# Hi/lo splits of streamed weights: all on the Vector engine, none on GpSimd

## The chip, the core and the metric

One core of a Trainium2 chip runs the whole program. The metric is device time in microseconds (us) for one execution; the profiled execution is taken by the hardware profiler. Engines are named as in the profile: PE is TensorE's matmuls, DVE is VectorE, ACT is ScalarE, POOL is GpSimd, SP issues the loads.

## What is computed

A trunk of four post-norm layers over 512 tokens of width 1024, in float32. Layer 0 mixes tokens with latent attention (MLA), layer 1 with retention, layer 2 with gated linear attention (GLA), layer 3 with MLA again. A SwiGLU feed-forward network (FFN, hidden width 2816) follows each mixer. Cut to what matters:

```python
for i in range(4):
    y = (mla, retention, gla)[i % 3](x)
    x = layer_norm(ALPHA * x + y)
    x = layer_norm(ALPHA * x + (silu(x @ Wg) * (x @ Wu)) @ Wo)
```

So there are eight sub-layers, and seven places where one sub-layer's LayerNorm is followed by the next sub-layer's first products.

## The kernel before

Every float32 product is made of three fast products. An operand x is split into hi (a rounded copy) and lo = x - hi, and `mm3` (L127) issues hi·hi, lo·hi and hi·lo into one PSUM sum (L128, L129, L130). Activations are split once, when they are made: x is kept transposed as `xh` and `xl`. Weights stream from memory and are split as they come. `wload` (L106) takes one of three raw buffers (`wraw`, `nraw=3`), has SP load 512 KB into it, and calls `wsplit` (L116): ACT copies to `whi` (L102), then a subtraction writes `wlo` (L103). There are six pairs of `whi` and `wlo` (`nhl=6`). A raw buffer is free for the next load when its subtraction is done, and a pair is free when the last matmul on it is done.

The subtraction runs on DVE, except for some weights that `wsplit` gives to POOL, by a counter:

```python
self.split(hi, lo, raw, self.nc.gpsimd if self.relieve > 0 else None)
self.relieve -= 1
```

The counter `relieve` is set to 6 at the end of a sub-layer (L228 in `out_proj`, the short output projection of retention, GLA and FFN; L260 in `out_tail`, that of MLA) and to 2 in three turns of GLA's loop over heads (L1060). The next so many weights go to POOL: six behind each of seven sub-layers (behind the eighth there are no weights left) and two in each of three turns of GLA, 48 in all. POOL's other work (four additions per pair of FFN columns, L329 to L332; part of retention's output, L899 and L900; the root of MLA's normalisation; set-up of GLA, L950 to L960 and L1077) does not depend on the counter.

LayerNorm works on four tiles of 128 tokens. When the last output sum of a tile is ready in PSUM, DVE adds it into `xt` (`acc`, L182 or L184) and takes statistics (L186). `ln_finish` then runs on DVE: mean and variance (L191), a reciprocal root as a chain of one-column steps (L141 to L149, tiles `lnx`, `lny`, `lnu`), two steps (x - mean)·g (L205, 512 columns each) and two steps ·r + b (L206). Then PE transposes the tile (L158), ACT copies it to `xh`, and DVE subtracts to get `xl` (L103). The next sub-layer's first products on that tile need `xh`, `xl` and the split weights. The work is staggered: while tile 2 or 3 is normalised, PE ends the old sub-layer or works on the tiles that are done.

The order of each engine's queue is fixed when the program is built: a scheduler goes through the program with its own estimate of durations and puts the next ready instruction into its engine's queue. On the chip every engine works its queue in that order and waits for what an instruction needs.

Of the kernel before, what the change touches and what calls it, by code (L numbers as in the profile page):

```python
# [9 lines left out]
F32 = mybir.dt.float32  # L10
# [3 lines left out]
ALU = mybir.AluOpType  # L14
# [36 lines left out]
class Trunk:  # L51
    def __init__(self, tc, ctx, ins, nb=47, nraw=3, nhl=6):
        self.tc, self.nc, self.ins = tc, tc.nc, ins
        nc = tc.nc
        ctx.enter_context(nc.allow_non_contiguous_dma(reason="rows of weights and broadcasts"))
        pool = lambda name, bufs, **k: ctx.enter_context(tc.tile_pool(name=name, bufs=bufs, **k))
        self.cp = pool("cp", 1)
        self.wp = pool("wp", 1)
        self.nb = nb
        self.sp = pool("sp", 8)  # L60
        self.lnp = pool("lnp", 2)

        xp = pool("xp", 1)
        self.xh = xp.tile([P, KT, S], F32R, name="xh")
        self.xl = xp.tile([P, KT, S], F32R, name="xl")
        self.ps_pool = pool("psum", 6, space=bass.MemoryType.PSUM)
        self.nraw, self.nhl = nraw, nhl
        self.relieve = 0
        self.pending = []
        self.waiting = []  # L70

        self.ident = self.cp.tile([P, P], F32, name="ident")
        make_identity(nc, self.ident)
        self.xt = [self.cp.tile([P, D], F32, name=f"xt{t}") for t in range(NT)]
# [23 lines left out]
        return self.b(shape, F32R, "bh", tag), self.b(shape, F32R, "bl", tag)  # L98


    def split(self, hi, lo, src, eng=None):
        a = self.nc.scalar.copy(hi, src)  # L102
        b = (eng or self.nc.vector).tensor_tensor(lo, src, hi.bitcast(F32), op=ALU.subtract)  # L103
        return a.ins, b.ins

    def wload(self, srcs, a, n):  # L106
# [9 lines left out]
    def wsplit(self, raw, a, n):  # L116
        hi = self.wp.tile([P, a, n], F32R, tag="whi", name="whi", bufs=self.nhl)
        lo = self.wp.tile([P, a, n], F32R, tag="wlo", name="wlo", bufs=self.nhl)
        self.split(hi, lo, raw, self.nc.gpsimd if self.relieve > 0 else None)
        self.relieve -= 1  # L120
        return hi, lo

    def wcols(self, w, r0, kt, c0, n):
# [89 lines left out]
    def out_proj(self, st, w, nf, coef, last, out=None, halves=(0, 1)):  # L213
        wf = lambda f0, half: self.wcols(w, f0 * P, 2, half * 512, 512)
        if nf <= 6:
            ch = {(c, hf): wf(2 * c, hf) for hf in halves for c in range(nf // 2)}
            for t in range(NT):
                for hf in halves:
                    ps = self.ps()
                    for f in range(nf):  # L220
                        if last and hf == 0 and f == 3:
                            self.flush(t - 2)
                        w2 = ch[f // 2, hf]
                        self.mm3(ps, st(f, t), (w2[0][:, f % 2, :], w2[1][:, f % 2, :]), f == 0, f == nf - 1)
                    self.acc(t, hf, ps, coef, last)
                if last:
                    self.ln_finish(t, out)
            self.relieve = 6 if last else 0  # L228
            return
        pss = [self.ps() for _ in range(NT)]  # L230
        for f in range(nf):
            if f % 2 == 0:
                w2 = wf(f, 0)
            for t in range(NT):
                self.mm3(pss[t], st(f, t), (w2[0][:, f % 2, :], w2[1][:, f % 2, :]), f == 0, f == nf - 1)
        for t in range(NT):
            self.acc(t, 0, pss[t], coef, last)
        self.out_tail(st, lambda f0: wf(f0, 1), nf, coef, last, out)

    def out_tail(self, st, wf, nf, coef, last, out=None):  # L240

        pss = [self.ps() for _ in range(NT)]
        nl = 8
        for f in range(nf - nl):
            if f % 2 == 0:
                w2 = wf(f)
            for t in range(NT):
                self.mm3(pss[t], st(f, t), (w2[0][:, f % 2, :], w2[1][:, f % 2, :]), f == 0, False)
        ch = [wf(nf - nl + 2 * c) for c in range(nl // 2)]
        for t in range(NT):  # L250
            for c in range(nl):
                if last and c == 3:
                    self.flush(t - 2)
                f = nf - nl + c
                w2 = ch[c // 2]
                self.mm3(pss[t], st(f, t), (w2[0][:, c % 2, :], w2[1][:, c % 2, :]), f == 0, f == nf - 1)
            self.acc(t, 1, pss[t], coef, last)
            if last:
                self.ln_finish(t, out)
        self.relieve = 6  # L260


    def proj_f(self, w2, ps, kt, m, c=slice(None), mid=None):
# [680 lines left out]
    def gla(self, l, j):  # L944
# [22 lines left out]
        def values(h):  # L967

            v = self.bpair((P, 2, 256), "v"), self.bpair((P, 2, 256), "v")
            put = lambda t, ps: self.split(v[t // 2][0][:, t % 2], v[t // 2][1][:, t % 2], ps[:, :256])  # L970
            return [(v[t // 2][0][:, t % 2], v[t // 2][1][:, t % 2]) for t in range(NT)], 1024 + h * 256, put

        def gate(h):
            r = self.b((P, 2, 256), tag="r"), self.b((P, 2, 256), tag="r")
            return r, 2048 + h * 256, lambda t, ps: nc.scalar.copy(r[t // 2][:, t % 2], ps[:, :256])

        def project(*parts):
            ws = [self.proj_w(w, c0, 256, 4) for _, c0, _ in parts]
            for t in range(NT):
                for wk, (_, _, put) in zip(ws, parts):  # L980
                    self.proj_tile(t, wk, 256, put)
            return [p[0] for p in parts]
# [33 lines left out]
        def out(pr, yT, last, halves=(0, 1)):  # L1016
            if last:
                self.ln_begin(l, 0)
            st = lambda f, t: (yT[f][0][:, t * P : (t + 1) * P], yT[f][1][:, t * P : (t + 1) * P])
            coef = ALPHA if pr == 0 else None  # L1020
            self.out_proj(st, wo[pr * 512 : (pr + 1) * 512], 4, coef, last, halves=halves)

        def silu(r):
            for x in r:
                self.silu = self.tc.keep_in_program_order(nc.scalar.activation(x, x, AF.Silu))
# [17 lines left out]
        for h in range(GLA_H):  # L1043
            at, states = self._gla_scores(c, keys, v, fwd, crs)
            if h < 2:
                if h:
                    qk["q", h + 2] = q(h + 2)
                qk["k", h + 2] = k(h + 2)
            else:
                out(0, yT[:4], False, (h - 2,))  # L1050
            self._gla_mix(at, states, c[2:], v, r, ng)
            r0 = r
            if h + 1 < GLA_H:
                cs = gates(h + 1)
                c = self._gla_chain(cs, qk["q", h + 1], qk["k", h + 1])
                (v,) = project(values(h + 1))
            yT += self._gla_turn(r0)
            if h + 1 < GLA_H:
                (r,) = project(gate(h + 1))
                self.relieve = 2  # L1060
                keys = self._gla_keys(c)
                silu(r)
        out(1, yT[4:], True)
# [238 lines left out]
```

## Time and profile before

| | us |
|---|---|
| median of 3 runs (2597.5 to 2599.05) | 2598.49 |
| the profiled execution's own time | 2597.42 |
| its span, first to last instruction | 2595.6 |
| PE busy | 2539.5 |
| DVE busy | 1798.4 |
| ACT busy | 975.8 |
| POOL busy | 328.3 |

A row of the timeline gives start, duration, engine, line, operation, the tiles written and read, and in brackets how long the engine sat idle before it and what it waited for. "x2" means that two like instructions are merged, and the duration is that of both. A row of the windows gives for a stretch (from:to) its length, then each engine's busy time with its count of instructions, the granted clock of PE as a share of the full one (PEclk), the share of the DMA engines and GB/s.

### The profile page before, as it was taken

How to read it: one execution, taken by the hardware profiler on the slowest of the kernel's cores; microseconds unless marked ns; L12 is line 12 of the kernel's file. 1: busy time of each engine (PE TensorE's matmuls, PEld its weight loads, DVE VectorE, ACT ScalarE, POOL GpSimd, SP SyncE). 2: the span in 40 equal slices, each digit the busy share in tenths (PEclk: the TensorE clock that was granted, in tenths of full speed). 3: DMA queues.
4: the chain of work that ended last, by engine and by line, in shares of the span. 5: the costliest groups of instructions: out<-in, count | busy, mean ns of one | idle time of the engine just before them, and what ended most of it. 6: DMA issues, size and time to landing. Idle time of an engine off the chain costs nothing.

```text
span 2595.6 us, 32600 instructions
## 1 busy us (share of the span) xinstructions
PE 2539.5 (98%) x12804; PEld 2159.8 (83%) x12804; DVE 1798.4 (69%) x2932; ACT 975.8 (38%) x1405; POOL 328.3 (13%) x327
## 2 busy tenths in 40 slices
PE   8999999999999999999999999999999999999998
PEld 7788888887888887988888998888888788888886
DVE  6877766668655648666657888876657686676656
ACT  4652333323333332333323665233332564233331
POOL 3002111002100103111102001211101200211101
PEclk9999999999999999999999999999999999999999
DMA  4213333323222323323322222333332221333331
GB/s 146 74 42 94 106 98 97 102 77 98 81 82 77 102 75 89 114 91 107 111 94 83 82 66 74 110 98 98 97 90 79 78 68 47 117 97 98 98 90 57
DMA packets 294714, 232.36 MB, mean 90 GB/s; under 512 B 21120, under 2 KB 244480, under 8 KB 294560
## 3 DMA queue, kind: packets, MB, share of 16 engines
q1 hardware_dynamic: 294560, 230.28, 29.3%
q8 instruction: 100, 1.64, 0.3%
q14 instruction: 54, 0.44, 0.1%
HBM read 228.15 MB, written 2.10 MB: 89 GB/s over the span
## 4 chain that ended last, share of the span: by engine, by line
PE 88%; DVE 9%; ACT 2%; DMA 1%; POOL 1%; issue 1%; DVEq 0%; SPq 0%; ACTq 0%; POOLq 0%
PE ps L128 28%; PE ps L130 28%; PE ps L129 28%; DVE xt L205 2%; DVE xt L206 1%; PE tp L663 1%; DVE lnst L186 1%; PE tp L158 1%; DVE lnu L145 1%; PE ps L644 1%; DVE xt L182 1%; DVE xl L103 1%; PE ps L643 0%; DVE wlo L103 0%; ACT whi L102 0%
## 5 line engine op out<-in xcount | busy, mean ns | idle before, releaser
L102 ACT CAST whi<-wraw 128x1024 fp32r<-128x1024 f32 (+3 forms) x398 | 412.1, 1040 | 700.4 <-issue 251.6
L129 PE MATMUL ps<-xl,whi 128*128 128x512 f32 (+1 forms) x1792 | 659.1, 368 | 8.6 <-DVE xl L103 8.6
L128 PE MATMUL ps<-xh,whi 128*128 128x512 f32 (+1 forms) x1792 | 659.3, 368 | 0.0
L130 PE MATMUL ps<-xh,wlo 128*128 128x512 f32 (+1 forms) x1792 | 658.4, 367 | 0.0
L103 DVE TENSOR_TENSOR wlo<-wraw,whi 128x1024 fp32r<-128x1024 f32 (+2 forms) x350 | 431.1, 1242 | 204.8 <-ACT whi L102 197.2
L129 PEld LDWEIGHTS ps<-xl,whi 128*128 128x128 f32 x1792 | 340.1, 190 | 64.6 <-DVE xl L103 9.6
L128 PEld LDWEIGHTS ps<-xh,whi 128*128 128x128 f32 x1792 | 340.2, 190 | 55.0 <-issue 0.4
L130 PEld LDWEIGHTS ps<-xh,wlo 128*128 128x128 f32 x1792 | 340.1, 190 | 54.5
L130 PE MATMUL ps<-whi,xl 128*128 128x512 f32 (+3 forms) x752 | 265.2, 353 | 5.5 <-DVE xl L103 5.5
L128 PE MATMUL ps<-whi,xh 128*128 128x512 f32 (+3 forms) x752 | 267.0, 355 | 0.7 <-ACT xh L102 0.7
L129 PE MATMUL ps<-wlo,xh 128*128 128x512 f32 (+3 forms) x752 | 264.9, 352 | 2.0 <-POOL wlo L103 2.0
L103 POOL TENSOR_TENSOR wlo<-wraw,whi 128x1024 fp32r<-128x1024 f32 (+4 forms) x48 | 118.2, 2478 | 927.1 <-ACT whi L102 916.0
L182 DVE TENSOR_TENSOR xt<-ps,xt 128x512 f32<-128x512 f32 x288 | 187.3, 683 | 35.5 <-PE ps L130 35.5
L128 PE MATMUL ps<-whi,fh 128*128 128x512 f32 x448 | 174.3, 389 | 0.0
L129 PE MATMUL ps<-wlo,fh 128*128 128x512 f32 x448 | 174.3, 389 | 0.0
L130 PE MATMUL ps<-whi,fl 128*128 128x512 f32 x448 | 174.3, 389 | 0.0
L130 PEld LDWEIGHTS ps<-whi,xl 128*128 128x128 f32 x752 | 144.8, 193 | 23.7 <-DVE xl L103 6.5
L129 PEld LDWEIGHTS ps<-wlo,xh 128*128 128x128 f32 x752 | 144.8, 193 | 19.2 <-POOL wlo L103 2.2
L128 PEld LDWEIGHTS ps<-whi,xh 128*128 128x128 f32 x752 | 144.8, 193 | 18.5 <-ACT xh L102 1.1
L326 DVE TENSOR_TENSOR ft<-ps,b 128x512 f32<-128x512 f32 x64 | 44.2, 691 | 142.0 <-PE ps L130 77.8
L102 ACT CAST whi<-wt 128x1024 fp32r<-128x1024 f32 x64 | 67.5, 1054 | 190.9 <-PE ps L129 128.3
L128 PE MATMUL ps<-bh 128*128 128x256 f32 (+1 forms) x376 | 124.1, 335 | 6.0 <-ACT bh L102 5.5
(259 smaller groups left out, 4041.7 us busy)
## 6 DMA issues: line engine op xcount, KB each, us to landing
wraw<-in_ffn_w_in SPq DMA_DIRECT2D x176, 512.0 KB, 3.9
wt<-in_ffn_w_out SPq DMA_DIRECT2D x48, 512.0 KB, 4.7
wraw<-in_ret_w_in SPq DMA_DIRECT2D x48, 512.0 KB, 3.9
wraw<-in_ffn_w_out SPq DMA_DIRECT2D x40, 512.0 KB, 3.3
wraw<-in_gla_w_in SPq DMA_DIRECT2D x22, 512.0 KB, 3.6
wraw<-in_mla_w_o SPq DMA_DIRECT2D x16, 512.0 KB, 3.8
wraw<-in_ret_w_o SPq DMA_DIRECT2D x16, 512.0 KB, 4.7
wraw<-in_mla_w_down SPq DMA_DIRECT2D x8, 512.0 KB, 4.5
```

The costliest lines, as they stand in the source:

```text
L102: a = self.nc.scalar.copy(hi, src)
L103: b = (eng or self.nc.vector).tensor_tensor(lo, src, hi.bitcast(F32), op=ALU.subtract)
L128: mm(out, s[0], m[0], start=start, stop=False)
L129: mm(out, s[0], m[1], start=False, stop=False)
L130: mm(out, s[1], m[0], start=False, stop=stop)
L145: stt(u, y, y, x, op0=ALU.mult, op1=ALU.mult)
L158: nc.tensor.transpose(ps[:, j, :], self.xt[t][:, (4 * g + j) * P : (4 * g + j + 1) * P], self.ident)
L182: nc.vector.tensor_tensor(x, ps, x, op=ALU.add)
L186: nc.vector.bn_stats(self.stats[t][:, half * 6 : half * 6 + 6], x)
L205: nc.vector.scalar_tensor_tensor(x[:, sl], x[:, sl], mv[:, 0:1], self.g[:, sl], op0=ALU.subtract, op1=ALU.mult)
L206: nc.vector.scalar_tensor_tensor(x[:, sl], x[:, sl], r, self.bb[:, sl], op0=ALU.mult, op1=ALU.add)
L326: nc.vector.tensor_tensor(ft[:, 2:4, :] if f % 2 else ft[:, 1::-1, :], half(pu), half(s), op=ALU.mult)
```

## The change

The counter goes, and with it the choice of engine in `split`: all weights' subtractions are issued to DVE. LayerNorm and everything else stay as they are.

```diff
-        self.relieve = 0
...
-    def split(self, hi, lo, src, eng=None):
+    def split(self, hi, lo, src):
         a = self.nc.scalar.copy(hi, src)
-        b = (eng or self.nc.vector).tensor_tensor(lo, src, hi.bitcast(F32), op=ALU.subtract)
+        b = self.nc.vector.tensor_tensor(lo, src, hi.bitcast(F32), op=ALU.subtract)
         return a.ins, b.ins
...
     def wsplit(self, raw, a, n):
...
-        self.split(hi, lo, raw, self.nc.gpsimd if self.relieve > 0 else None)
-        self.relieve -= 1
+        self.split(hi, lo, raw)
...
-            self.relieve = 6 if last else 0
...
-        self.relieve = 6
...
-                self.relieve = 2
```

## Rows read from the trace of the kernel before

**Rows 1.** Windows: the end of the first MLA, and the FFN behind it.
```profile
205.00:262.00 57.00, 54.09 (x326) 47.70 (x325) 46.93 (x90) 14.49 (x19) 15.02 (x6) 1.00 0.35 107
262.00:585.00 323.00, 323.00 (x1503) 270.64 (x1502) 215.40 (x261) 106.81 (x115) 29.06 (x32) 1.00 0.32 97
```

**Rows 2.** Timeline of PE, the instructions behind its ten longest waits at these places.
```profile
242.90 0.39 PE L129 MATMUL ps<-xl,whi 128*128 128x256 f32 x1 [2.26 <-DVE xl L103]
...
615.78 0.80 PE L130 MATMUL ps<-whi,xl 128*128 128x512 f32 x1 [4.91 <-DVE xl L103]
...
1037.43 0.46 PE L129 MATMUL ps<-xl,whi 128*128 128x256 f32 x1 [3.42 <-DVE xl L103]
...
1398.71 0.40 PE L129 MATMUL ps<-wlo,xh 128*128 128x288 f32 x1 [1.96 <-POOL wlo L103]
...
1590.39 1.85 PE L1159 MATMUL tp<-ident,b 128*128 128x128 f32 x8 [1.81 <-DVE bl L103]
...
1616.84 0.44 PE L1240 MATMUL tp<-ident,b 128*128 128x128 f32 x2 [2.31 <-DVE b L1233]
...
1642.55 0.63 PE L158 MATMUL tp<-ident,xt 128*128 128x128 f32 x4 [1.77 <-DVE xt L206]
...
1654.39 1.43 PE L158 MATMUL tp<-ident,xt 128*128 128x128 f32 x8 [3.62 <-DVE xt L206]
...
2013.31 0.63 PE L158 MATMUL tp<-ident,xt 128*128 128x128 f32 x4 [2.13 <-DVE xt L206]
...
2232.44 0.58 PE L129 MATMUL ps<-xl,whi 128*128 128x256 f32 x1 [2.26 <-DVE xl L103]
```

**Rows 3.** Costliest groups of the page: the weights' subtraction on DVE and on POOL.
```profile
L103 DVE TENSOR_TENSOR wlo<-wraw,whi 128x1024 fp32r<-128x1024 f32 (+2 forms) x350 | 431.1, 1242 | 204.8 <-ACT whi L102 197.2
...
L103 POOL TENSOR_TENSOR wlo<-wraw,whi 128x1024 fp32r<-128x1024 f32 (+4 forms) x48 | 118.2, 2478 | 927.1 <-ACT whi L102 916.0
```

**Rows 4.** Two LayerNorm lines over the whole run: count, ns least/median/most.
```profile
L205 DVE SCALAR_TENSOR_TENSOR xt<-xt,lnmv,ln_g x61: 737/743/2939, 224.3 to 2588.4; 128x512 f32<-128x512 f32 x61
...
L145 DVE SCALAR_TENSOR_TENSOR lnu<-lny,lnx x32: 206/215/2356, 225.6 to 2589.1; 128x1 f32<-128x1 f32 x32
```

**Rows 5.** Timeline of DVE and POOL, from the first FFN to retention.
```profile
591.55 2.94 DVE L205 SCALAR_TENSOR_TENSOR xt<-xt,lnmv,ln_g 128x512 f32<-128x512 f32 x1
594.41 2.36 DVE L145 SCALAR_TENSOR_TENSOR lnu<-lny,lnx 128x1 f32<-128x1 f32 x1
...
602.46 5.12 DVE L206 SCALAR_TENSOR_TENSOR xt<-xt,lny,ln_b 128x512 f32<-128x512 f32 x2
...
591.53 9.94 POOL L103 TENSOR_TENSOR wlo<-wraw,whi 128x1024 fp32r<-128x1024 f32 x4 [110.28 <-ACT whi L102]
```

**Rows 6.** Timeline of DVE and POOL, from the first MLA to its FFN.
```profile
237.18 2.84 DVE L205 SCALAR_TENSOR_TENSOR xt<-xt,lnmv,ln_g 128x512 f32<-128x512 f32 x1
...
245.11 1.81 DVE L147 SCALAR_TENSOR_TENSOR lny<-lnu,lny 128x1 f32<-128x1 f32 x1
...
236.70 10.21 POOL L103 TENSOR_TENSOR wlo<-wraw,whi 128x1024 fp32r<-128x1024 f32 x4 [16.16 <-ACT whi L102]
```

**Rows 7.** Timeline of DVE, from GLA to its FFN.
```profile
1638.88 3.52 DVE L206 SCALAR_TENSOR_TENSOR xt<-xt,lny,ln_b 128x512 f32<-128x512 f32 x2
...
1644.90 2.88 DVE L205 SCALAR_TENSOR_TENSOR xt<-xt,lnmv,ln_g 128x512 f32<-128x512 f32 x1
```

**Rows 8.** Windows behind three of the waits, for the granted clock.
```profile
614.00:622.00 8.00, 6.22 (x19) 4.98 (x20) 2.92 (x5) 0.01 (x1) 0.00 (x0) 0.57 0.01 2
1037.00:1042.00 5.00, 4.57 (x25) 4.57 (x26) 5.00 (x11) 0.00 (x0) 2.08 (x1) 0.66 0.84 251
...
2232.00:2237.00 5.00, 4.56 (x26) 4.56 (x27) 4.89 (x7) 1.05 (x1) 4.44 (x2) 0.66 0.71 200
```

**Rows 9.** Waits of ACT for loads: 585 to 640 us, and whole run (total, times, longest).
```profile
ACT whi L102 <- DMA wraw<-in_ret_w_in: 7.4, 4, 2.7
...
ACT whi L102 <- DMA wraw<-in_ffn_w_in: 14.2, 6, 3.9
```

## The prediction

> **What bounds the kernel now.** I read the windows by stage first. Between the ends of sub-layers PE never rests: 323.00 of 323.00 us in the first FFN, at a full clock [rows 1]. There no other engine can add or save time, unless it becomes so late that PE waits. What is to be had lies at the ends and inside GLA, so I went through PE's timeline there and took the ten long waits [rows 2]. The reader is to see who is waited for: nine times DVE (the subtraction `xl`, the LayerNorm step L206 ahead of a transpose, two chains of GLA), once POOL's own subtraction `wlo`. They sum to 26.5 us: 2.26 + 4.91 + 3.42 + 1.96 + 1.81 + 2.31 + 1.77 + 3.62 + 2.13 + 2.26.
>
> Then I asked why DVE is late. The LayerNorm steps have two durations: L205 takes 0.74 us as a rule but 2.94 at most, and L145, one column wide, 0.21 as a rule but 2.36 at most [rows 4]. The long ones lie under POOL's subtractions. POOL begins four at 591.53, L205 is issued at 591.55 and takes 2.94, L145 behind it 2.36 [rows 5]; the same with POOL's four from 236.70 [rows 6]. A one-column step that ends about when a POOL instruction of 2.5 us ends has not computed for 2 us: it was held. So each POOL subtraction (2.48 us) can cost DVE up to its whole duration, where DVE's own subtraction of the same tile costs 1.24 [rows 3].
>
> Last, what a wait does to PE afterwards. In the window behind the longest, the granted clock is 0.57 of the full one, that is, the lower level of 1.2 GHz for most of it; behind seven others it is the same for a shorter time, with 0.66 in the first and in the last of them [rows 8]. Full clock came back after PE had worked again. The first window lost 8 x 0.43 = 3.4 us, of which about 0.8 was still waiting: 2.6. The others lost 5 x 0.34 = 1.7 each. Two of the ten waits, 2.26 at 242.90 [rows 2] among them, had no drop: its window has 1.00 throughout [rows 1].
>
> **The change part by part.** It removes 48 subtractions from POOL and adds 48 to DVE: 48 x 2.48 = 118 us of POOL, 48 x 1.24 = 60 us of DVE [rows 3]. In busy time this is nothing for PE, for most ends have gaps and DVE is at 46.93 of 57 us even with the holds counted in [rows 1]. What counts is the chain at each end.
>
> *First FFN to retention (wait 4.91).* L205 lost 2.94 - 0.74 = 2.2, L145 2.36 - 0.21 = 2.1, two more chain steps about 1.6 each (1.81 against 0.2, as the last held step of rows 6), the pair L206 5.12 - 1.48 = 3.6 [rows 4 to 6]: 11.1 us held. Six DVE subtractions put back 6 x 1.24 = 7.4. Even if all six stand ahead of the late `xl`, the chain is 3.7 earlier. I take 3.7.
>
> *First MLA to FFN (2.26).* Four steps were held, from 2.84 to 1.81 [rows 6]: 2.1 + 2.1 + 1.6 + 1.6 = 7.4, against four subtractions, 5.0. The other two of the six fall in DVE's gaps before. The 2.4 that is left covers the wait: 2.26 gone. The second MLA has the same rows and the same wait: 2.26.
>
> *FFN to the second MLA (2.13).* The pattern of the first FFN's end, with six splits: the 3.7 covers it, 2.13 gone.
>
> *FFN to GLA (1.96).* PE waits for POOL's `wlo` itself [rows 2], which stands in POOL's queue behind GLA's set-up. On DVE it leaves that queue: 1.96 gone.
>
> *GLA to FFN (1.77 + 3.62).* The pair L206 lost 3.52 - 1.48 = 2.0, two L205 2.1 each [rows 7]: 6.2, against four subtractions, 5.0. At the least 1.2 of 5.39 goes; I take this.
>
> *Retention to FFN (3.42), and GLA's two waits (1.81, 2.31).* One subtraction of 1.24 for a hold of up to 2.48: half of each, 1.7 + 0.9 + 1.2.
>
> Sum of waits: 3.7 + 2.26 + 2.26 + 2.13 + 1.96 + 1.2 + 1.7 + 0.9 + 1.2 = 17.3 us. Below that I could go to half of all, 13.2; above, to all 26.5.
>
> *The clock.* Where the wait goes, the slow stretch should go: behind 1398.71, 2013.31 and 2232.44, 3 x 1.7 = 5.1. The one behind 615.78 too (2.6), since the 1.2 us of wait that stays is less than the 2.26 that had no drop. Behind retention and in GLA I leave it. Together 7.7; ends are 0 and 2.6 + 7 x 1.7 = 14.5.
>
> *Queues.* A split issues no load, but its end frees one of three raw buffers, so SP's next load starts when the subtraction ends: 1.2 us sooner, or later if DVE has it far back in its queue. Costed at nothing: the FFN has slack on DVE, and at the ends it is the third rival. POOL's remaining work only moves forward.
>
> Total 17.3 + 7.7 = 25.0. The profiled execution took 2597.42, 1.07 under the median; 2598.49 - 25.0 = 2573.5.
>
> **The rivals.** *More than forecast:* all ten waits and all slow stretches go, 26.5 + 14.5 = 41.0: 2557.5. For it: in the trace DVE runs far behind PE there, and the gains add up from tile to tile. Against: four splits still come in one LayerNorm chain.
>
> *Less:* the splits go into the gaps between the chain's steps, ahead of what PE waits for, and half of each wait stays, with its slow stretches: 2598.49 - 13.2 = 2585.3. For it: the order is the scheduler's, which lets ready work into such gaps.
>
> *No change:* DVE is simply full at the ends, at 46.93 of 57 us [rows 1], and what the holds gave up the splits take: about 2598. Against it stands 11.1 held for 7.4 added. Here a page speaks against the change. The Trainium skill ("Perfetto Trace Analysis", Optimizing Scalar/DVE Operations) says that with DVE saturated, giving some of its work to GpSimd may make sense, though it warns of an SBUF port that the two share. By the first half of that rule the time would be as in this rival or worse; the trace bears out the warning, since DVE loses more to POOL's subtractions than doing them would cost, 11.1 against 7.4 at the first FFN's end.
>
> *Slower:* DVE is in order, and a split needs ACT's cast, which needs the load. On POOL that waiting hurt nobody. At retention's start ACT waited four times for loads, 7.4 us, and for FFN weights 14.2 us in all [rows 9]. If DVE's queue has these splits ahead of the LayerNorm of tiles 2 and 3, it stands as long: 7.4 at each of three mixers' starts and 14.2 make 36.4. Less the 17.3, with all slow stretches kept: 2598.5 + 19.1 = 2617.6. It decides from about half of the 36.4 on. Against: raw buffers come free sooner, so the casts come sooner too.
>
> That the change does nothing is excluded: `wsplit` is the only caller that named an engine.
>
> **How the numbers follow.** Forecast 0.46, more 0.15, less 0.17, no change 0.10, slower 0.12. A measurement here can tell about 0.2%, 5.2 us. Faster by over that: 0.46 + 0.15 + 0.17 = 0.78; same 0.10; slower 0.12. The range holds forecast, more and less with their unknown parts, and part of no change: from 2557 to 2596. The slower rival is left out.
>
> **What would show it.** POOL's `wlo` rows are gone and DVE's are 48 more. No L205 over 1 us and no L145 over 0.3 at the ends. PE's waits at retention's start, GLA's start and both MLA ends under 1 us, and a full clock behind them. I would be wrong if DVE shows `wlo` waits for `whi` of 2 us and more inside the LayerNorm chains, or if L205 stays long without POOL.

## The result, and the profile after

The changed kernel takes 2556.28 us (median of 4 runs, 2555.73 to 2556.84) beside 2597.99 us of the kernel before (4 runs): a ratio of 0.9843, with a 95% interval of 0.9829 to 0.9858. That is 41.7 us less. The forecast was 25.0 less, the rival *more* 41.0. The new kernel's lines stand one to five higher up: L102 is the subtraction, L143 the one-column step, L203 and L204 LayerNorm's wide steps, L180 and L182 the sums into `xt`.

The first part of the page of the changed kernel, busy time by engine:

```profile
PE 2524.5 (99%) x12804; PEld 2147.2 (84%) x12804; DVE 1776.7 (70%) x2980; ACT 976.8 (38%) x1405; POOL 212.4 (8%) x279
```

POOL lost its 48 splits (327 instructions to 279). DVE got 48 more and is nevertheless busy for 21.7 us less than before: the time for which it was held was counted as busy, and there was more of it than the 60 us of new splits.

Windows of the changed kernel at three of the ends (columns as in [rows 1]), and behind them those of the kernel before for the second and the third. The third lies 24.6 us later there, since the kernel before has fallen behind by that much:

```profile
205.00:262.00 57.00, 57.00 (x358) 51.40 (x357) 48.30 (x102) 14.39 (x19) 0.00 (x0) 1.00 0.35 107
585.00:640.00 55.00, 54.36 (x252) 44.90 (x251) 45.17 (x99) 22.76 (x29) 2.60 (x2) 1.00 0.39 117
...
1590.00:1640.00 50.00, 49.94 (x328) 44.57 (x327) 47.56 (x136) 11.93 (x23) 0.00 (x0) 1.00 0.33 101
...
585.00:640.00 55.00, 49.67 (x220) 40.65 (x219) 45.62 (x88) 19.61 (x25) 16.87 (x8) 0.94 0.32 96
1614.60:1664.60 50.00, 42.34 (x238) 36.59 (x239) 45.31 (x120) 9.82 (x15) 11.12 (x5) 0.93 0.32 98
```

PE is now busy nearly all through them (0.64 us of the second is a wait), at the full clock. The first answers to [rows 1], where it was 54.09 of the same 57 us. All of PE's waits in the changed kernel from 195 to 2540 us (total, times, longest):

```profile
PE ps L126 <- ACT bh L101: 3.3, 5, 1.6
PE ps L128 <- DVE xl L102: 0.6, 1, 0.6
PE tp L659 <- DVE mx L643: 0.5, 1, 0.5
PE tp L532 <- DVE b L526: 0.3, 1, 0.3
```

They are 4.7 us; the same view of the kernel before adds up to 31.8. Nine of the ten waits of [rows 2] are gone. Of the longest, the 4.91 us for `xl` at retention's start, 0.64 is left:

```profile
608.25 0.50 PE L128 MATMUL ps<-whi,xl 128*128 128x512 f32 x1 [0.64 <-DVE xl L102]
```

The two LayerNorm lines of [rows 4] (count, ns least/median/most):

```profile
L143 DVE SCALAR_TENSOR_TENSOR lnu<-lny,lnx x32: 207/214/222, 226.8 to 2548.8; 128x1 f32<-128x1 f32 x32
...
L203 DVE SCALAR_TENSOR_TENSOR xt<-xt,lnmv,ln_g x61: 739/742/752, 225.5 to 2548.2; 128x512 f32<-128x512 f32 x61
```

The medians are the same, the long ones are gone: 222 where it was 2356, 752 where it was 2939. And where did the new splits go? DVE's timeline from the first FFN to retention, beside [rows 5], and one row of POOL:

```profile
591.00 1.22 DVE L102 TENSOR_TENSOR wlo<-wraw,whi 128x1024 fp32r<-128x1024 f32 x1
...
592.93 1.22 DVE L102 TENSOR_TENSOR wlo<-wraw,whi 128x1024 fp32r<-128x1024 f32 x1
594.07 1.41 DVE L204 SCALAR_TENSOR_TENSOR xt<-xt,lny,ln_b 128x512 f32<-128x512 f32 x2
...
596.59 1.21 DVE L102 TENSOR_TENSOR wlo<-wraw,whi 128x1024 fp32r<-128x1024 f32 x1
...
598.32 1.21 DVE L102 TENSOR_TENSOR wlo<-wraw,whi 128x1024 fp32r<-128x1024 f32 x1
...
600.21 1.23 DVE L102 TENSOR_TENSOR wlo<-wraw,whi 128x1024 fp32r<-128x1024 f32 x1 [0.56 <-ACT whi L101]
...
603.65 1.22 DVE L102 TENSOR_TENSOR wlo<-wraw,whi 128x1024 fp32r<-128x1024 f32 x1
604.79 0.90 DVE L145 SCALAR_TENSOR_TENSOR lny<-lnu,lny 128x1 f32<-128x1 f32 x1
...
607.51 1.28 DVE L102 TENSOR_TENSOR xl<-tp,xh 128x512 fp32r<-128x512 f32 x2
...
603.97 1.71 POOL L770 CAST ret_di<-ret_di 128x896 f32<-128x896 int32 x1
```

The splits do stand inside the LayerNorm chains, between the small steps. Tile 2's last steps (L204) have two ahead of them and take 1.41 us, where the pair took 5.12. The subtraction `xl` at 607.51, for which PE waits here, has all six ahead of it. The waiting for a cast that the fourth rival feared is 0.56 us; inside the chains of the other ends it is 0.81 at most. One small step is still long: L145 at 604.79 takes 0.90 us, where 0.15 is usual, and ends at 605.69. A conversion that POOL has to do in any case ends at 605.68.

### The profile page after: what moved, and what is told of

Same layout as the page of the kernel before. It is cut to its first block, busy times and chain, and to the rows that moved or that the text cites. A ratio compares the mean times of both kernels' runs of the same rounds, so it can differ in the third digit from the quotient of the medians.

```text
span 2554.2 us, 32600 instructions
## 1 busy us (share of the span) xinstructions
PE 2524.5 (99%) x12804; PEld 2147.2 (84%) x12804; DVE 1776.7 (70%) x2980; ACT 976.8 (38%) x1405; POOL 212.4 (8%) x279
## 4 chain that ended last, share of the span: by engine, by line
PE 93%; DVE 3%; ACT 2%; DMA 1%; issue 1%; POOL 1%; SPq 0%; DVEq 0%; ACTq 0%; POOLq 0%
PE ps L126 30%; PE ps L127 30%; PE ps L128 30%; PE tp L659 1%; PE tp L156 1%; DVE wlo L102 1%; PE ps L640 1%; PE ps L639 0%; ACT whi L101 0%; DMA wraw<-in_mla_w_ukv 0%; DMA wraw<-in_mla_w_down 0%; DMA wraw<-in_ret_w_in 0%; ACT bh L101 0%; ACT b L549 0%; PE tp L903 0%
## 5 line engine op out<-in xcount | busy, mean ns | idle before, releaser
L102 DVE TENSOR_TENSOR wlo<-wraw,whi 128x1024 fp32r<-128x1024 f32 (+3 forms) x398 | 487.6, 1234 | 212.5 <-ACT whi L101 205.1
L180 DVE TENSOR_TENSOR xt<-ps,xt 128x512 f32<-128x512 f32 x288 | 187.2, 682 | 34.9 <-PE ps L128 34.9
L325 POOL TENSOR_TENSOR ft<-ft 128x256 f32<-128x256 f32 x32 | 24.6, 770 | 1466.9 <-DVE ft L322 1466.9
```

The source lines that it names most:

```text
L102: b = self.nc.vector.tensor_tensor(lo, src, hi.bitcast(F32), op=ALU.subtract)
L180: nc.vector.tensor_tensor(x, ps, x, op=ALU.add)
L325: tt(ft[:, 4, :], ft[:, 0, :], ft[:, 3, :], op=ALU.add)
```

## The experiments

Three theories could explain the same time. H: a POOL subtraction holds DVE's two-input steps while it runs. S: nothing is held in a way that matters, but POOL delivers a split in 2.48 us for 1.24, so weights and raw buffers come late. O: the scheduler's new queue order is the gain. Where no run of the changed kernel stands beside an experiment on its chip, I compare with 0.9845 times the kernel before there (the ratio that the changed kernel had when it was run again, below).

### dum_read: the holds without the splits

The changed kernel with the old counter back, which now only adds dummy work on POOL:

```diff
+        self.idle = self.cp.tile([P, 512], F32, name="idle")
+        nc.gpsimd.memset(self.idle, 0.0)
...
         self.split(hi, lo, raw)
+        if self.relieve > 0:
+            self.nc.gpsimd.tensor_copy(self.idle[:, :1], hi.bitcast(F32)[:, 0, :1])
+            for _ in range(2):
+                self.nc.gpsimd.tensor_tensor(self.idle, self.idle, self.idle, op=ALU.subtract)
+        self.relieve -= 1
```

> The changed kernel, all 48 splits on DVE, plus dummy work on POOL at the 48 places where a split stood before: a one-column copy from the weight tile, then two 512-column subtractions on a scratch tile (about 2.6 us in all, reading and writing SBUF). Nothing waits for the dummies and PE's and DVE's queues are almost as in the changed kernel. Theory H (POOL instructions hold DVE): the LayerNorm steps are long again, one-column steps of over 1 us at the ends, PE's waits and slow-clock stretches come back, now with the splits on DVE as well: 2590 to 2620 us. Rival S (a split on POOL was slow to deliver, 2.48 us for 1.24, so weights and raw buffers came late) and rival O (the new kernel gains by its other queue order): as the changed kernel, 2556 +- 3 us, no long step.

Measured: 2603.04 us, ratio to the kernel before 1.0029 (1.0017 to 1.0041). That is some 47 us above the changed kernel, on nearly its queues (by the traces, 16 of DVE's 2980 instructions and 9 of PE's 12804 stand elsewhere). The one-column step, the statistics step (one input) and POOL's dummies, in the groups by line (count, ns least/median/most):

```profile
L151 DVE SCALAR_TENSOR_TENSOR lnu<-lny,lnx x32: 206/216/1000, 225.0 to 2595.3; 128x1 f32<-128x1 f32 x32
...
L192 DVE BATCH_NORM_STATS2 lnst<-xt x64: 640/694/696, 215.6 to 2592.8; 128x6 f32<-128x512 f32 x64
...
L125 POOL TENSOR_TENSOR idle<-idle x96: 1037/1042/2043, 211.9 to 2243.4; 128x512 f32<-128x512 f32 x96
```

The timeline of DVE and POOL at the first MLA's end:

```profile
237.20 1.00 DVE L151 SCALAR_TENSOR_TENSOR lnu<-lny,lnx 128x1 f32<-128x1 f32 x1
...
236.69 2.62 POOL L125 TENSOR_TENSOR idle<-idle 128x512 f32<-128x512 f32 x2
```

PE's two longest groups of waits in the whole run:

```profile
PE tp L164 <- DVE xt L212: 10.8, 10, 2.1
PE ps L135 <- DVE wlo L105: 9.9, 6, 2.8
```

PE and DVE wait for no dummy, and still the steps are long and PE waits again, for the same tiles as in [rows 2] and now for DVE's own `wlo` too. S and O said 2556 and fall as the main cause; H stands. (S keeps one of the ten waits of [rows 2], the 1.96 us for POOL's own `wlo`.) The hold now comes on top of the splits, so the kernel is slower than before.

### dum_write: the same time of POOL, but only writing

As dum_read, with other dummies behind the one-column copy:

```diff
-            for _ in range(2):
-                self.nc.gpsimd.tensor_tensor(self.idle, self.idle, self.idle, op=ALU.subtract)
+            for _ in range(5):
+                self.nc.gpsimd.memset(self.idle, 0.0)
```

> As dum_read, but the dummies are five 512-column memsets (about 2.6 us, writing SBUF and reading nothing), behind the same one-column copy. Theory H in its wide form (any POOL instruction holds DVE): as dum_read, 2590 to 2620 us. Theory H in its narrow form (only a POOL instruction that reads SBUF holds a two-input DVE step): 2556 +- 3 us, L143-like one-column steps stay at 0.2 us. S and O: 2556 +- 3.

Measured: 2557.68 us, ratio 0.9852 (0.9838 to 0.9867), not told apart from the changed kernel. The one-column step, and POOL's dummies, in the groups by line:

```profile
L151 DVE SCALAR_TENSOR_TENSOR lnu<-lny,lnx x32: 207/214/220, 226.9 to 2551.5; 128x1 f32<-128x1 f32 x32
...
L125 POOL MEMSET idle<- x240: 515/526/827, 213.8 to 2205.8; 128x512 f32 x120
```

POOL was as busy (356.7 us in the whole run, 364.0 in dum_read) at the same places, and no step of LayerNorm was long. So H holds in its narrow form: it is POOL's reading that holds DVE. The Trainium skill says so ("SBUF — State Buffer", Who interferes with whom): a DVE instruction with two SBUF inputs and a GpSimd instruction that reads SBUF exclude each other, one that only writes does not. The two runs agree, 1000 ns against 220 for the same step; so does the statistics step, which has one input and was never held (696 at most, above).

### dum_copy: reading with one input

As dum_read, with other dummies again:

```diff
-            for _ in range(2):
-                self.nc.gpsimd.tensor_tensor(self.idle, self.idle, self.idle, op=ALU.subtract)
+            for _ in range(6):
+                self.nc.gpsimd.tensor_copy(self.idle[:, :256], self.idle[:, 256:])
```

> As dum_read, but the dummies are six 256-column copies on POOL (one SBUF input each, about 2.5 us). If any POOL instruction that reads SBUF holds two-input DVE steps: 2590 to 2605 us, as dum_read (2603). If only two-input POOL instructions hold them: 2556 +- 3, as dum_write (2558). The copies are shorter each than a 512-column subtraction, so single holds are shorter.

Measured: 2571.82 us, ratio 0.9907 (0.9893 to 0.9920), between the two. The step and the copies, in the groups by line:

```profile
L151 DVE SCALAR_TENSOR_TENSOR lnu<-lny,lnx x32: 205/217/354, 226.2 to 2565.2; 128x1 f32<-128x1 f32 x32
...
L125 POOL COPY idle<-idle x288: 397/403/1489, 213.1 to 2224.7; 128x256 f32<-128x256 f32 x144
```

PE's longest wait in this run, at the second MLA's start, what DVE waited for ahead of it, and POOL's last dummies there:

```profile
2004.51 0.64 PE L136 MATMUL ps<-whi,xl 128*128 128x320 f32 x1 [7.79 <-DVE xl L105]
...
2001.11 0.48 DVE L536 TENSOR_SCALAR b<-ps,rmsy 128x256 f32<-128x256 f32 x1 [9.68 <-POOL rmsy L155]
...
1995.02 2.70 POOL L125 COPY idle<-idle 128x256 f32<-128x256 f32 x6
```

The time says little here. The copies took up to 1489 ns, POOL's queue grew long, and a root of MLA's normalisation (`rmsy`) stood in it behind the dummies, which ended at 1997.72. DVE waited 9.68 us for the root, the `xl` behind that in DVE's queue came late, and PE waited 7.79 us for it. That is late delivery, of the kind that S means, and not a hold.

The step's row can be used: copies do hold, and the step takes 0.35 us at most with copies of 0.40 (one other step of a chain took 0.57). So the longest step is about as long as a single POOL instruction: 2.36 us with splits of 2.48, 1.00 with subtractions of 1.04, 0.35 with copies of 0.40. I read from it that a hold lasts for what is left of the one instruction; no run varies that length alone.

### mid_ffn: 48 splits on POOL, elsewhere

The kernel before, with the counter set to 6 in the FFN's loop, at the column blocks 8 and 14, and nowhere else:

```diff
...
+            if f in (8, 14):
+                self.relieve = 6
```

> 48 splits on POOL as before the change, but in the middle of the four FFNs (six from hidden column block 8 and six from block 14 of each), none at the ends of sub-layers or in GLA. PE's order is that of the changed kernel. Theory H: DVE is held there too, but has 100 us of slack in an FFN of 323, so PE does not wait: 2556 +- 4 us, with held DVE steps in the trace. Rival S: late splits make PE wait in the FFN too, up to 1.24 us each: 2570 to 2610.

Measured: 2555.73 us, ratio 0.9848 (0.9833 to 0.9863). The first row of its page, and PE's wait for `xl` in its waits:

```profile
PE 2524.8 (99%) x12804; PEld 2147.8 (84%) x12804; DVE 1735.2 (68%) x2932; ACT 975.7 (38%) x1405; POOL 332.0 (13%) x327
...
PE ps L130 <- DVE xl L103: 1.3, 2, 0.8
```

DVE is held here too: it is busy for 41.5 us less than in the changed kernel, although splits of 60 us went to POOL, which leaves some 18 us of holding. But PE, whose queue has the changed kernel's order to the last instruction, waits for `xl` for 1.3 us in the whole run, with none of the long waits of [rows 2]. S expected 2570 and more: a split that comes 1.2 us later costs nothing here, where PE does not need it at once. The same 48 splits cost 41 us or nothing, by their place alone.

### p_ffn, p_mla, p_retgla, p_turns: one place at a time

The kernel before, with the counter set at one kind of place: behind FFNs, behind MLAs, behind retention and GLA, or in GLA's turns. The first:

```diff
-            self.relieve = 6 if last else 0
+            self.relieve = 6 if last and nf == 6 else 0
...
-        self.relieve = 6
+        self.relieve = 0
...
-                self.relieve = 2
```

> The kernel before with POOL splits only behind the first three FFNs (18 of 48). If each place brings its own cost, this adds to the changed kernel the waits and slow-clock stretches seen there in the trace before: waits 4.91 + 0.42 + 1.96 + 2.13 + 0.63 = 10.1 us, clock 2.6 + 1.7 + 1.7 = 6.0: 2572 us (2569 to 2576). Rival (queue order as a whole, not the place, made the difference): 2556 +- 3 or 2598.

> POOL splits only behind the two MLAs (12 of 48). Sum of the place: waits 2.26 + 0.65 + 2.26 = 5.2, clock 1.7: 2563 us (2560 to 2566). Rival: 2556 +- 2, or 2598.

> POOL splits only behind retention and GLA (12 of 48; two of GLA's six lie inside its last turn). Sum of the place: waits 3.42 + 2.31 + 1.77 + 3.62 = 11.1, clock 3 x 1.7 = 5.1: 2572 us (2568 to 2576). Rival: 2556 +- 2, or 2598.

> POOL splits only in GLA's three turns (6 of 48). Sum of the place: wait 1.81, clock 1.7: 2560 us (2557 to 2562). Rival: 2556 +- 1. The four places together should give 10.1 + 6.0 + 5.2 + 1.7 + 11.1 + 5.1 + 1.8 + 1.7 = 42.7 us, the whole difference.

| POOL splits | us | ratio to before (95%) | above 2555.9 | expected above 2556 |
|---|---|---|---|---|
| behind FFNs | 2570.80 | 0.9904 (0.9889 to 0.9919) | 14.9 | 16 |
| behind MLAs | 2565.87 | 0.9885 (0.9870 to 0.9900) | 10.0 | 7 |
| behind retention and GLA | 2571.61 | 0.9907 (0.9893 to 0.9922) | 15.7 | 16 |
| GLA's turns | 2558.33 | 0.9854 (0.9838 to 0.9871) | 2.4 | 4 |

2555.9 is 2596.16 (the kernel before beside them) times 0.9845. The four add to 43.0 us, against 40.2 for all together; each has an interval of some 4 us either way. Each place brings its own waits back. PE's waits in p_ffn, from 200 to 2545 us:

```profile
PE ps L130 <- DVE xl L103: 4.9, 1, 4.9
PE tp L158 <- DVE xt L206: 3.3, 3, 2.1
...
PE ps L129 <- POOL wlo L103: 2.0, 1, 2.0
```

The same in p_retgla, and one group each of p_mla and p_turns:

```profile
PE tp L158 <- DVE xt L206: 5.4, 2, 3.6
PE ps L129 <- DVE xl L103: 3.4, 1, 3.4
...
PE tp L1239 <- DVE b L1232: 2.3, 1, 2.3
...
PE ps L129 <- DVE xl L103: 5.8, 4, 2.2
...
PE tp L1159 <- DVE bl L103: 1.8, 1, 1.8
```

They are those of [rows 2] at the same places, to a tenth. Waits of 10.2 us in p_ffn go with 14.9 us of time (12.8 in the execution that was profiled); the rest I put down to the lower clock behind them. The MLAs' 10.0 is 3 us above expectation; the interval does not tell that from none.

### dum_dve: how much room DVE has at the ends

As dum_read, with the dummies on DVE:

```diff
-            self.nc.gpsimd.tensor_copy(self.idle[:, :1], hi.bitcast(F32)[:, 0, :1])
-                self.nc.gpsimd.tensor_tensor(self.idle, self.idle, self.idle, op=ALU.subtract)
+            self.nc.vector.tensor_copy(self.idle[:, :1], hi.bitcast(F32)[:, 0, :1])
+                self.nc.vector.tensor_tensor(self.idle, self.idle, self.idle, op=ALU.subtract)
```

> The changed kernel with dummy work on DVE at the 48 places: a one-column copy and two 512-column subtractions on scratch (about 1.4 us). It asks what 48 splits on DVE cost there. My prediction's term (splits stand in the LayerNorm chains at full price and hold PE in part): as many again cost 10 to 20 us, 2566 to 2576. Theory F (DVE has free time behind what PE waits for, so a split there costs PE nothing): 2555 to 2561 us.

Measured: 2569.24 us, ratio 0.9898 (0.9884 to 0.9911): 13.9 us above the changed kernel on the same chip, for 48 times 1.5 us of dummies. Theory F, that work there is free for DVE, falls for this load. The longest of PE's waits from 200 to 2545 us (the next are 2.1 and 1.8):

```profile
PE tp L164 <- DVE xl L105: 2.9, 1, 2.9
```

The first 48 splits leave no long wait, as many dummies on top of them do: DVE's room at the ends is about used up by the change. (Some 200 of DVE's instructions also stand elsewhere in its queue here, so part of the 13.9 may be order.)

### after_again and v_rms: the same lesson once more

In the changed kernel the largest wait left that DVE makes is at the start, for a root that POOL computes in the first MLA. A kernel with `nc.gpsimd` taken out of that call as well, which serves both MLAs:

```diff
-            return self.rsqrt(ss, 1.0 / n, RMS_EPS, "rmv" if t == NT - 1 else "rms", None if t == NT - 1 else nc.gpsimd)
+            return self.rsqrt(ss, 1.0 / n, RMS_EPS, "rmv" if t == NT - 1 else "rms")
```

> The changed kernel, and the reciprocal roots of MLA's two normalisations on DVE for all token tiles (before: on POOL for three tiles of four). In the changed kernel one POOL chain runs from 40.1 to 45.7 us, DVE stands behind it, and PE waits 4.4 us at 47.3, with a slow-clock stretch of 6.8 us around. If that chain sets the wait: 2548 to 2552 us. Rival (DVE is full there with the rotary tables and the chain's eight steps only get in their way): 2555 to 2560.

> The changed kernel once more, beside v_rms_again on the same chip: 2552 to 2557 us, ratio to the kernel before 0.984.

> The changed kernel with all of MLA's reciprocal roots on DVE, as in v_rms. It was 6 us under the changed kernel of another chip; if the start's wait (4.4 us and part of a slow-clock stretch) is what goes, 5 to 7 us under after_again here. Rival (the two chips differ): within 2 us of it.

Measured: v_rms 2549.59, ratio 0.9823 (0.9806 to 0.9839). Beside each other on one chip: the changed kernel 2555.38 (0.9845, 0.9831 to 0.9858), v_rms again 2549.36 (0.9821, 0.9807 to 0.9834), 6.0 us less; the runs of the two don't overlap (2554.73 and more, 2549.54 and less). In the changed kernel's timeline, a step of POOL's chain, what DVE does meanwhile, DVE's step that waits for the chain's end, and PE's wait for DVE:

```profile
41.90 1.78 POOL L143 TENSOR_SCALAR rmsu<-rmsy,rmsx 128x1 f32<-128x1 f32 x1
...
41.73 1.22 DVE L102 TENSOR_TENSOR wlo<-wraw,whi 128x1024 fp32r<-128x1024 f32 x1
42.87 0.68 DVE L467 TENSOR_TENSOR tab<-tab,rope 128x512 f32<-128x512 f32 x1
...
45.73 0.75 DVE L516 TENSOR_SCALAR b<-ps,rmsy 128x512 f32<-128x512 f32 x1 [0.91 <-POOL rmsy L147]
...
47.26 0.69 PE L532 MATMUL tp<-ident,b 128*128 128x128 f32 x2 [4.36 <-DVE b L526]
```

Here it is POOL that is held: its one-column step takes 1.78 us, where 0.34 is the least for that line. It begins while DVE works on two inputs and ends at 43.68, just behind DVE's second such instruction (43.55). DVE and PE wait behind it. In v_rms the longest wait of that stretch is

```profile
57.18 0.76 PE L532 MATMUL tp<-ident,b 128*128 128x128 f32 x5 [1.47 <-DVE b L516]
```

This version is the fastest of the study.

## Why the prediction was right, and where it was too small

**The mechanism** was right. POOL's subtractions held DVE's LayerNorm steps, PE waited for DVE, and eight of the ten waits were followed by a stretch at the lower clock. The long steps are gone with the splits, but for one of 0.90 us under other work of POOL; they come back with dummies that read (dum_read) and not with dummies that write, and place by place the costs add up.

**The size** was short by 16.7 us: 41.7 against 25.0. The measured 2556.28 lies at the very end of the range that I gave, 2557 to 2596: 0.7 us beneath it, or, as the ratio times the 2598.49 that I started from, at 2557.7. Two terms make nearly all of it. The waits: I took part of four groups where nearly all went. From GLA to its FFN I wrote "At the least 1.2 of 5.39 goes; I take this"; behind retention and in GLA "half of each", 3.8 of 7.54; at retention's start 3.7 of 4.91. That leaves 4.2 + 3.7 + 1.2 = 9.1 us, and 0.64 is what stayed: 8.5 too little. The clock: with those waits I left their slow stretches, 7.7 of 14.5, another 6.8. Together 15.3; three waits that I had not counted, 0.42, 0.63 and 0.65 us, went too. The price of the clock is borne out by its mean: 0.992 over 2595.6 us and 0.998 over 2554.2 make an estimate of 16 us for all stretches, beside 14.5.

**The term that was too small** is the price of the new splits against what the holds gave back. I took a lower bound for the forecast: the splits ahead of the step that PE waits for, at full price, and behind retention and in GLA one hold for one split. The rows show something else, place by place. Behind retention PE waited 3.42 us for the `xl` at 1036.70 in the kernel before. Two long steps lie ahead of that, and in the changed kernel no split stands ahead of the same `xl` (1023.13); the first comes behind it:

```profile
1031.73 2.83 DVE L205 SCALAR_TENSOR_TENSOR xt<-xt,lnmv,ln_g 128x512 f32<-128x512 f32 x1
1034.48 2.29 DVE L145 SCALAR_TENSOR_TENSOR lnu<-lny,lnx 128x1 f32<-128x1 f32 x1
1036.70 0.68 DVE L103 TENSOR_TENSOR xl<-tp,xh 128x512 fp32r<-128x512 f32 x1
...
1023.13 0.68 DVE L102 TENSOR_TENSOR xl<-tp,xh 128x512 fp32r<-128x512 f32 x1
...
1025.85 1.22 DVE L102 TENSOR_TENSOR wlo<-wraw,whi 128x1024 fp32r<-128x1024 f32 x1
```

So 4.2 us were held there and nothing was put back. From GLA to its FFN none of the four splits stands ahead of the steps for which PE waited 1.77 us, and two stand ahead of those for which it waited 3.62: 2.3 us put back for 6.2 held. At retention's start all six do stand ahead of the `xl`, as I had assumed, and there the term was near: 4.3 us went, where I had 3.7. I had counted too little as held (the last pair L206 took 2.15 us for 1.41 as well), and a split takes 1.14 us of DVE's queue, since the next instruction starts before it ends (592.93 to 594.07). At the first MLA's end the 2.26 was right by a wrong account, which is luck: two of the four long steps lie ahead of the `xl` that PE waited for, and no split does. What decides is where the scheduler puts the splits, and that I did not work out. dum_dve shows that the fear was not idle: as much work again does cost 14 us.

**The rivals.** *More*, to which I gave 0.15, is what happened, 41.0 against 41.7. *Less* falls: one wait of [rows 2] is left in part, 0.64 of 4.91. *No change*, DVE full at the ends, falls for this change; with about twice the load some of it comes true (dum_dve). *Slower*, DVE standing at ACT's casts, has its place in the rows (0.56 us, 0.81 at most) but not its price, 7.4 us at one start: of the six splits shown above five did not wait at all.

**The signs** named were all there: 48 rows of `wlo` moved, no L203 over 0.752 us, no L143 over 0.222 in LayerNorm, 0.64 us at most of wait at the four ends, a clock of 1.00 behind them.

## What to carry to other kernels

Before giving elementwise work to GpSimd, look at what VectorE does at the same moment: a GpSimd instruction that reads SBUF held VectorE's two-input steps for the rest of its own duration, and a step of 0.2 us in a serial chain took 2.4. The same offload was free in the middle of an FFN and cost 41 us behind the ends of sub-layers and in GLA's loop, where a chain of small steps on VectorE is what the matmuls wait for. So the sign to look for is one form of instruction with two durations, and the other engine's instruction that ends with the long one.

## What was not expected of the hardware

- Memsets on GpSimd, 240 of 0.53 us at the same places, held nothing: the one-column step stayed at 0.22 us at most.
- The hold goes both ways. With DVE busy, POOL's 256-column copies took 1.49 us at most for 0.40, and a one-column step of POOL 1.78.
- The held step's length followed the single POOL instruction, not the total: 2.36, 1.00 and 0.35 us at most with instructions of 2.48, 1.04 and 0.40.
